# One ordered chain on GpSimd's queue, with a release by ScalarE per step, for the transfers that sum weight blocks in DRAM

## The chip, the cores and the metric

The kernel is one layer of a decoder block and runs on one core of a Trainium2 chip. The metric is the device time of one execution in microseconds. A core has TensorE (PE, matmul), VectorE (DVE), ScalarE (ACT), GpSimd (POOL) and SyncE (SP); each runs its own instructions in order and waits on semaphores for the others. Transfers are issued by an engine (here SP, GpSimd, seldom ScalarE) and carried out by 16 transfer engines that all issuers share.

## The reference

Sequence 512, width 1024, one sequence, float32 throughout. What matters for the change is the second half of the layer, a gated FFN with an inner width of 2816:

```python
    x = x + gate1 * (merged @ w_out)
    h2 = rms_norm(x, norm2_g) * (1.0 + scale2) + shift2
    f_g, f_u = jnp.split(h2 @ w_ffn_in, 2, axis=-1)
    x = x + gate2 * ((jax.nn.silu(f_g) * f_u) @ w_ffn_out)
    return x
```

The gates, scales and shifts come from `silu(c) @ w_ada + b_ada`, one vector of 1024 per section. A final RMSNorm follows.

## The kernel before, in words

**Products.** A float32 product is made of three matmuls on rounded halves: each operand is split into a rounded part (`hi`, made by ScalarE, a copy with rounding) and the rest (`lo`, a subtraction on VectorE). On top of that the larger products are done in the Strassen-Winograd way: seven products of half-size blocks in place of eight, with sums of blocks as operands.

**The first FFN projection** (lines 1623 to 1699) is a loop over `q` from -2 to 17, twenty iterations, each for 256 columns of `w_ffn_in`; even `q` makes the part that goes through SiLU, odd `q` the part that is multiplied by it. An iteration has seven calls of `sprod` (12 matmuls each) into PSUM tiles `R[0]` to `R[3]`. Between them stand, in the order of the code, ScalarE's copies of one PSUM tile into the next (`R[1] <- R[0]`, L1657, `R[2] <- R[1]`, L1670) and into SBUF (`ps`, L1665, L1677), VectorE's sums out of PSUM (L1682, L1685), and the steps that prepare the weights of the next iteration (`s_prep`: `a0`, `a1`, `a2`, `a3` on ScalarE at L1324, L1335, L1345 and L1352; `d0` to `d3` on VectorE at L1327 to L1355). The raw weights of the iteration after next (1 MB, tile `raw`) are loaded by SP at the head of the iteration (`s_issue`, L1298).

**Modulation.** In the iterations with `q` from 1 to 8, `last_mod` does one eighth of the last modulation vector: VectorE multiplies a tile `mraw` of `w_ada` and adds it to `acc` (L175, L177). Every second time SP first loads two such tiles (L205, 512 KB each); they reuse one buffer, so a load starts when the accumulation before it is done.

**Sums of weight blocks.** The second FFN projection is done in seven block products as well, and four of its right operands are sums of blocks of `w_ffn_out`. These sums don't pass through an engine. They are made in DRAM while the first projection runs, in four arrays `wsum[1]` to `wsum[4]`, each cut into `NZ` = 5 blocks of 256x512 (512 KB). For one block `c`, with B(i,j) the block in half i of the rows and half j of the columns, `wsum_steps` (line 292) lists six steps:

1. copy B(0,0) to `wsum[1]` and B(0,1) to `wsum[3]`
2. add B(0,1) to `wsum[1]` and B(1,1) to `wsum[3]`
3. copy `wsum[1]` to `wsum[2]`
4. add B(1,1) to `wsum[2]`
5. copy `wsum[2]` to `wsum[4]`
6. add B(1,0) to `wsum[4]`

That is eight transfers a block. A copy is issued by SP (L307), an addition is an accumulating transfer issued by GpSimd (L305). A step that reads or adds to what an earlier one wrote waits for it on the issuing engine.

**Order around the change.** The program order is the order of the code on every engine. `wstep` (line 318) takes the next entry of the list `wsteps`, if there is one, and calls it; it stands at two places in an iteration, after the third `sprod` (line 1669) and at the end (line 1697), so there are forty places. Before the change the blocks go in pairs: steps 1 of blocks 0 and 1, steps 2 of blocks 0 and 1 and so on (12 places), then blocks 2 and 3 (12 places), then block 4 with an empty place after each step (12 places). Neither SP nor GpSimd waits for the place itself: SP issues a copy when it comes to it in its own queue, and GpSimd an addition when the transfer before it has landed.

**After the loop** the second projection loads its weights through `raw` (L92), partly from `w_ffn_out` and partly from the four arrays, in the order plain, sum 1, sum 2, plain, sum 3, two plain blocks, sum 4, plain. GpSimd loads the gain of the final norm (L1774) and takes powers for the row norms (L1235).

`sm` is a tile of 128x64 for small per-row values; columns 0 to 19 are in use. `cols` holds small constants, loaded at the start.

Of the kernel before, what the change touches and what calls it, by code (L numbers as in the profile page):

```python
# [12 lines left out]
AF = mybir.ActivationFunctionType  # L13
# [15 lines left out]
def block_kernel(ctx: ExitStack, tc: tile.TileContext, x, positions, w_ada, b_ada, w_in,  # L29
# [3 lines left out]
    T, V, A, P, SY = nc.tensor, nc.vector, nc.scalar, nc.gpsimd, nc.sync  # L33
# [116 lines left out]
    cols = base.tile([128, 59], F32, name="cols")  # L150
# [123 lines left out]
    wsum = {n: dram.tile([NZ * 256, 512], F32, name=f"wsum{n}") for n in (1, 2, 3, 4)}  # L274
# [17 lines left out]
    def wsum_steps():  # L292

        def step(c, *moves):
            o = slice(256 * c, 256 * c + 256)

            def fn():
                for n, add, src in moves:
                    if isinstance(src, tuple):
                        k = KZ[src[0]][2 * c] * 128  # L300
                        src = w_ffn_out[k:k + 256, 512 * src[1]:512 * src[1] + 512]
                    else:
                        src = wsum[src][o]
                    if add:
                        P.dma_start(wsum[n][o], src, accum_op=OP.add)  # L305
                    else:
                        SY.dma_start(wsum[n][o], src)  # L307
            return fn

        parts = [[step(c, *m) for m in (  # L310
            ((1, 0, (0, 0)), (3, 0, (0, 1))), ((1, 1, (0, 1)), (3, 1, (1, 1))), ((2, 0, 1),), ((2, 1, (1, 1)),),
            ((4, 0, 2),), ((4, 1, (1, 0)),))] for c in range(NZ)]
        return ([fn for c in (0, 2) for two in zip(parts[c], parts[c + 1]) for fn in two] +
                [fn for one in parts[4] for fn in (one, None)])

    wsteps = wsum_steps()

    def wstep():
        fn = wsteps.pop(0) if wsteps else None
        if fn:  # L320
            fn()
    assert next(mm_, None) is None
    sec_done = []
# [3 lines left out]
    for i in range(4):  # L327
        t = base.tile([128, D], F32, name=f"x{i}", tag=f"X{i}", bufs=1)
# [11 lines left out]
    sm = base.tile([128, 64], F32, name="sm")  # L340
# [1246 lines left out]
    for half in range(2):  # L1587
        o = slice(half * 256, (half + 1) * 256)
# [34 lines left out]
    for q in range(-2, NQ):  # L1623
# [42 lines left out]
        for fn in pre[1]:  # L1666
            fn()
        sprod(R[1], S2_, TB[2], False)
        wstep()
        A.activation(R[2], R[1], AF.Copy)  # L1670
        pre[2][0]()
# [21 lines left out]
        if q == 10:  # L1693
            for b_ in (3, 2):
                mbank[0] = b_
                sec_tasks(one=True)
        wstep()
        if q in (9, 13, NQ - 2):
            a_sum("S1", {9: 0, 13: 2}.get(q, 1))
# [103 lines left out]
    for h in range(2):  # L1803
        hi, lo = get(W_FO[h])
        for tk in range(4):
            o = (Z[h] if tk < 2 else Z[2 + h])[tk % 2]
# [31 lines left out]
    for tk in range(2):  # L1838
        for z in range(2) if tk else (None,):
            c = ALL if z is None else slice(256 * z, 256 * z + 256)  # L1840
            o = Z[1][0] if z is None else (Z[1][1][:, :256], last[:, :256])[z]
            for n_, w in enumerate(ch):
                zmm(o, "S4", 2 + n_, tk, w, c, False, n_ == 2)
            n = c.stop - c.start
# [62 lines left out]
```

## Time and profile before

| What | us |
|---|---|
| runs, median of 3 (lowest, highest) | 832.04 (831.22, 832.65) |
| profiled execution | 831.31 |
| its span | 829.5 |
| TensorE busy in it | 810.3 (98%) |
| VectorE busy | 684.5 (83%) |
| ScalarE busy | 427.0 (51%) |
| GpSimd busy | 126.7 (15%) |

The profile shows one execution. "Busy" leaves out the issuing of transfers on SP, and a busy TensorE is not always at its peak. In a timeline a row has the start and the length in us, the engine, the line of the code, the operation, the tile written and the tiles read, and in brackets the idle time before it with what ended it. In the rows of transfers `x4, 512.0 KB, 11.2` means four issues of 512 KB and the median time of 11.2 us from issue to landing. In the view by stretches each engine has its busy time and, in brackets, the number of instructions; then come the granted clock of TensorE as a share of full speed, the mean busy share of the 16 transfer engines, and GB/s.

### The profile page before, as it was taken

The numbers are of one execution on the slowest core, as the hardware profiler recorded it, in microseconds if no ns is written. First come the engines' busy times: TensorE is split into PE (matmuls) and PEld (weight loads), VectorE is DVE, ScalarE is ACT, GpSimd is POOL, SyncE is SP. The second block draws the span as 40 slices with busy tenths as digits, with TensorE's granted clock in tenths as the row PEclk, the third lists the DMA queues.
The fourth block names the chain that finished last, engine by engine and source line by source line (L and its number), as shares of the span: only waits on it lengthen the run. The fifth ranks groups of instructions, "written<-read, shape, count | busy, mean of one in ns | idle before, by whom it ended". The sixth has DMA issues, their size and how long they took to land.

```text
span 829.5 us, 12872 instructions
## 1 busy us (share of the span) xinstructions
PE 810.3 (98%) x4920; PEld 723.6 (87%) x4920; DVE 684.5 (83%) x1167; ACT 427.0 (51%) x730; POOL 126.7 (15%) x121
## 2 busy tenths in 40 slices
PE   7999999999999999999999999999899999999995
PEld 6889889988888888988888899999899999888784
DVE  7989788798899558886697869899699888897676
ACT  6674444323322236665536586555355556666543
POOL 2060032362353411000000001001000000000001
PEclk9999999999999999999999999999999999999999
DMA  9974352423345652057531409899998863556533
GB/s 296 310 203 118 102 178 77 118 87 101 124 137 176 197 178 77 26 157 243 185 102 50 154 28 257 222 271 295 254 265 208 199 162 125 178 189 195 177 129 126
DMA packets 108477, 138.46 MB, mean 167 GB/s; under 512 B 6480, under 2 KB 77136, under 8 KB 108256
## 3 DMA queue, kind: packets, MB, share of 16 engines
q1 hardware_dynamic: 99872, 120.24, 45.7%
q0 software_dynamic: 7824, 16.59, 10.4%
q8 instruction: 38, 0.62, 0.3%
q10 hardware_dynamic: 720, 0.82, 0.3%
q14 instruction: 23, 0.19, 0.1%
HBM read 135.26 MB, written 23.07 MB: 191 GB/s over the span
## 4 chain that ended last, share of the span: by engine, by line
PE 50%; DVE 18%; DMA 6%; ACT 2%; issue 2%; POOL 0%; POOLq 0%; ACTq 0%; DVEq 0%
PE R L53 6%; PE R L54 6%; PE R L55 6%; DMA mraw<-in_w_ada_dram 6%; PE pfo L55 3%; PE pfo L53 3%; PE pfo L54 3%; DVE acc L177 3%; DVE sco L713 2%; DVE m L709 2%; PE pb L53 2%; PE pb L55 2%; PE pb L54 2%; DVE lo L116 2%; PE po L54 2%
## 5 line engine op out<-in xcount | busy, mean ns | idle before, releaser
L112 ACT ACTIVATE hi<-raw 128x1024 fp32r<-128x1024 f32 (+2 forms) x103 | 107.0, 1040 | 105.3 <-PE pfo L55 34.3
L116 DVE TENSOR_TENSOR lo<-raw,hi 128x1024 fp32r<-128x1024 f32 (+2 forms) x67 | 81.1, 1214 | 29.1 <-ACT hi L112 28.9
L116 POOL TENSOR_TENSOR lo<-raw,hi 128x1024 fp32r<-128x1024 f32 x29 | 73.3, 2531 | 127.9 <-ACT hi L112 122.2
L53 PE MATMUL pb<-h,hi 128*128 128x512 f32 (+1 forms) x192 | 74.6, 389 | 0.0
L54 PE MATMUL pb<-h,hi 128*128 128x512 f32 (+1 forms) x192 | 74.0, 385 | 0.0
L55 PE MATMUL pb<-h,lo 128*128 128x512 f32 (+1 forms) x192 | 74.0, 385 | 0.0
L54 PE MATMUL pfo<-lo,za 128*128 128x512 f32 (+1 forms) x146 | 56.3, 385 | 0.3 <-DVE lo L116 0.3
L55 PE MATMUL pfo<-hi,za 128*128 128x512 f32 (+1 forms) x146 | 56.2, 385 | 0.0
L53 PE MATMUL pfo<-hi,za 128*128 128x512 f32 (+1 forms) x146 | 56.1, 385 | 0.0
L177 DVE SCALAR_TENSOR_TENSOR acc<-mraw,cols,acc 128x512 f32<-128x512 f32 x49 | 39.6, 808 | 18.9 <-DMA mraw<-in_w_ada_dram 17.9
L53 PE MATMUL R<-tb,hi 128*128 128x256 f32 x160 | 45.0, 281 | 2.9 <-ACT R L1670 2.1
L53 PE MATMUL R<-tb,sx 128*128 128x256 f32 x160 | 45.3, 283 | 0.9 <-ACT R L1657 0.8
L54 PE MATMUL R<-tb,sx 128*128 128x256 f32 x160 | 45.1, 282 | 0.0
L55 PE MATMUL R<-tb,sx 128*128 128x256 f32 x160 | 45.0, 281 | 0.0
L55 PE MATMUL R<-tb,lo 128*128 128x256 f32 x160 | 44.9, 281 | 0.0
L54 PE MATMUL R<-tb,hi 128*128 128x256 f32 x160 | 44.7, 279 | 0.0
L305 POOL DMA_DIRECT2D wsum<-in_w_ffn_out_dram x20 | 17.8, 908 | 172.7 <-DMA wsum<-wsum 115.3
L55 PEld LDWEIGHTS pb<-h,lo 128*128 128x128 f32 x192 | 36.0, 187 | 7.3
L54 PEld LDWEIGHTS pb<-h,hi 128*128 128x128 f32 x192 | 36.0, 188 | 6.9
L53 PEld LDWEIGHTS pb<-h,hi 128*128 128x128 f32 x192 | 36.0, 188 | 6.9
L1235 POOL TENSOR_TENSOR sm<-sm,mhalf 128x1 f32<-128x1 f32 x8 | 5.3, 662 | 217.6 <-DVE sm L1234 217.6
L54 PE MATMUL pav<-lo,h 128*128 128x256 f32 x128 | 35.8, 279 | 0.0
(373 smaller groups left out, 2643.6 us busy)
## 6 DMA issues: line engine op xcount, KB each, us to landing
raw<-in_w_ffn_in_dram SPq DMA_DIRECT2D x44, 512.0 KB, 6.5
raw<-in_w_in_dram SPq DMA_DIRECT2D x40, 512.0 KB, 3.8
mraw<-in_w_ada_dram SPq DMA_DIRECT2D x28, 512.0 KB, 4.0
wsum<-in_w_ffn_out_dram POOLq DMA_DIRECT2D x20, 512.0 KB, 9.3
raw<-wsum SPq DMA_DIRECT2D x20, 512.0 KB, 3.7
raw<-in_w_ffn_out_dram SPq DMA_DIRECT2D x18, 512.0 KB, 3.8
s<-in_w_ada_dram SPq DMA_DIRECT2D x30, 256.0 KB, 5.6
wsum<-in_w_ffn_out_dram SPq DMA_DIRECT2D x10, 512.0 KB, 8.6
```

What stands on the lines that cost most here:

```text
L53: T.matmul(o, wh, rh, start=start, stop=False, **kw)
L54: T.matmul(o, wh, rlo, start=False, stop=False, **kw)
L55: T.matmul(o, wlo, rh, start=False, stop=stop, **kw)
L112: A.activation(hi[:, :m], e["raw"][:, :m], AF.Copy)
L116: e["lo"].tensor_sub(lo[:, :m], e["raw"][:, :m], f(hi[:, :m]))
L177: V.scalar_tensor_tensor(o, w, cs[:, j:j + 1], o, op0=OP.mult, op1=OP.add)
L305: P.dma_start(wsum[n][o], src, accum_op=OP.add)
L709: V.max(m8s[i], sco[i])
L713: V.match_replace(out=sco[i], in_to_replace=m8s[i], in_values=sco[i], imm_value=TAKEN)
L1235: P.tensor_tensor(r2[:, tk:tk + 1], r2[:, tk:tk + 1], mhalf[:, :1], op=OP.pow)
```

## The change

Three things are changed in `wsum_steps` and `wstep`:

- The copies are issued by GpSimd, as the additions are. SP has none of these transfers any more.
- The order is one block after the other, six steps each, three steps and then an empty place. The thirty steps take all forty places, the last step the 39th.
- Ahead of each step ScalarE copies a column of 128 values (from `cols`) to a column of `sm` of the step's own, in 20 to 59, and GpSimd copies that column onto itself. GpSimd runs in order, so the step's transfers are issued after ScalarE has come to the step's place.

```diff
                     if add:
                         P.dma_start(wsum[n][o], src, accum_op=OP.add)
                     else:
-                        SY.dma_start(wsum[n][o], src)
+                        P.dma_start(wsum[n][o], src)
             return fn
...
-        return ([fn for c in (0, 2) for two in zip(parts[c], parts[c + 1]) for fn in two] +
-                [fn for one in parts[4] for fn in (one, None)])
+        order = sum(parts, [])
+        return [fn for k in range(0, len(order), 3) for fn in order[k:k + 3] + [None]]
 
     wsteps = wsum_steps()
 
     def wstep():
+
         fn = wsteps.pop(0) if wsteps else None
         if fn:
+            t = sm[:, 20 + len(wsteps):21 + len(wsteps)]
+            A.activation(t, cols[:, 58:59], AF.Copy)
+            P.tensor_copy(t, t)
             fn()
```

## The prediction

> **What bounds the kernel now.** I read the page first, then the matrix engine's time by stretches, then the instructions around the one stretch that is long, and last the transfers in flight there.
>
> ```profile
> PE 810.3 (98%) x4920; PEld 723.6 (87%) x4920; DVE 684.5 (83%) x1167; ACT 427.0 (51%) x730; POOL 126.7 (15%) x121
> ```
>
> TensorE is busy 98% of the span, so an edit can save only the time in which it stands still or runs slowly. The edit is in the twenty-iteration loop of the first FFN projection. I number its iterations 0 to 19 (the loop variable q is two less) and cut the trace at the first matmul of an iteration, the one on the tile `sa`; that of iteration 9 is:
>
> ```profile
> 598.90 0.28 PE L53 MATMUL R<-h,sa 128*128 128x256 f32 x1
> ```
>
> The view by stretches, cut so, for iterations 7 to 10:
>
> ```profile
> core 0: us, PE busy (x) PEld busy (x) DVE busy (x) ACT busy (x) POOL busy (x), PEclk, DMA share, GB/s
> 574.29:584.27 9.98, 9.98 (x86) 9.98 (x85) 9.23 (x13) 5.84 (x11) 2.65 (x3) 1.00 1.05 203
> 584.27:598.90 14.63, 11.74 (x86) 11.24 (x85) 8.09 (x14) 4.76 (x9) 0.48 (x1) 0.88 0.99 298
> 598.90:609.95 11.05, 10.25 (x86) 10.05 (x85) 10.64 (x14) 7.02 (x13) 1.28 (x2) 1.00 0.95 198
> 609.95:619.89 9.94, 9.94 (x86) 9.94 (x85) 9.45 (x15) 4.91 (x9) 0.88 (x1) 1.00 0.90 313
> ```
>
> A clean iteration takes 9.96 us (the mean of the first and last row). Iteration 8 takes 14.63 and iteration 9 11.05, with the same matmul count: 4.67 + 1.09 = **5.76 us** lost, part of it at a granted clock of 0.88. This is the loop's only stall on which the change can act. Who was late is in the timelines of ScalarE, TensorE and VectorE:
>
> ```profile
> 590.80 1.06 ACT L1335 ACTIVATE sx<-raw 128x1024 fp32r<-128x1024 f32 x1 [3.06 <-DMA raw<-in_w_ffn_in_dram]
> 591.76 0.37 ACT L1670 ACTIVATE R<-R 128x256 f32<-128x256 f32 x1
> 592.18 0.38 PE L53 MATMUL R<-tb,hi 128*128 128x256 f32 x1 [2.08 <-ACT R L1670]
> 592.49 0.49 DVE L175 TENSOR_SCALAR acc<-mraw,cols 128x512 f32<-128x512 f32 x1 [6.37 <-DMA mraw<-in_w_ada_dram]
> 595.73 1.06 ACT L1345 ACTIVATE sx<-raw 128x1024 fp32r<-128x1024 f32 x1 [3.61 <-DVE raw L1331]
> ```
>
> Two loads came late. ScalarE waited 3.06 us for a weight tile (`raw`), and the PSUM copy that TensorE needs (L1670) stood behind that wait; VectorE waited 6.37 us for a modulation tile (`mraw`), and through L1331 and L1345 that held ScalarE again. The chain of waits goes the same way; its longest piece in the loop is this transfer (start, length):
>
> ```profile
> 576.81 15.65 DMA mraw<-in_w_ada_dram
> ```
>
> What shared the transfer engines with it is in the timelines of SP's queue and GpSimd, and in the times to landing:
>
> ```profile
> 564.73 3.02 SPq L307 DMA_DIRECT2D wsum<-in_w_ffn_out_dram  x4
> 573.48 1.59 SPq L1298 DMA_DIRECT2D raw<-in_w_ffn_in_dram  x2
> 576.81 1.19 SPq L205 DMA_DIRECT2D mraw<-in_w_ada_dram  x2
> 572.97 0.88 POOL L305 DMA_DIRECT2D wsum<-in_w_ffn_out_dram  x1 [18.22 <-DMA wsum<-in_w_ffn_out_dram]
> 577.18 0.88 POOL L305 DMA_DIRECT2D wsum<-in_w_ffn_out_dram  x1 [0.42 <-issue]
> ```
>
> ```profile
> wsum<-in_w_ffn_out_dram POOLq DMA_DIRECT2D x4, 512.0 KB, 11.2
> raw<-in_w_ffn_in_dram SPq DMA_DIRECT2D x2, 512.0 KB, 13.8
> mraw<-in_w_ada_dram SPq DMA_DIRECT2D x2, 512.0 KB, 16.1
> mraw<-in_w_ada_dram SPq DMA_DIRECT2D x2, 512.0 KB, 10.9
> mraw<-in_w_ada_dram SPq DMA_DIRECT2D x2, 512.0 KB, 9.1
> ```
>
> The first three rows are issues between 571.5 and 579 us, the last two the loads of `mraw` in iterations 3 and 5. Two blocks of the weights' sums run side by side, so four copies and then four accumulating transfers (2 MB) fall together, and in iteration 7 those four meet 1 MB of weights and 1 MB of `mraw`. In iterations 3 and 5, beside two accumulating transfers, `mraw` lands in 9 to 11 us and no iteration is long.
>
> **The change part by part.** Three edits are made: the order (one block after the other, three steps in every four places), the queue (20 copies leave SP for GpSimd), and the gate (per step a 128x1 copy on ScalarE and one on GpSimd).
>
> Order: a step now holds two transfers at most, each waits for its predecessor, and a block takes 8 places, or four iterations: 4 x 9.96 = 39.8 us. What meets the `mraw` of iteration 7 is the second block's fourth step, one accumulating transfer, instead of four. How late may the loads be? VectorE was free for `mraw` 6.37 us before 592.49, at 586.12, or 9.3 us after its issue; the weight tile must let L1335 and L1670 (1.06 + 0.37) end by the fifth of seven products of iteration 8, 584.27 + 4/7 x 9.96 = 589.96, so it has to land by 588.5, some 14 us after its issue. With 9.1 to 10.9 us for `mraw`, VectorE is at most 1.6 us late, and of its 6.37 us here 2.8 never reached ScalarE (3.61); the weight tile has room. From below: nothing is saved if landing stays at 13.8 and 16.1; from above: all 5.76 us. I take all of it, since the traffic is below that of iterations 3 and 5.
>
> Queue: SP loses 20 issues and its waits for the accumulations; it is not on the path but it issues the weights. GpSimd gains 20 issues, priced by those it makes now.
>
> ```profile
> L305 POOL DMA_DIRECT2D wsum<-in_w_ffn_out_dram x20: 872/881/1307, 506.8 to 677.3; - x20
> L486 ACT ACTIVATE G<-modS,cols x8: 342/344/346, 15.8 to 51.7; 128x1 f32<-128x1 f32 x8
> L352 POOL TENSOR_SCALAR sm<-sm x4: 192/231/695, 6.5 to 12.3; 128x1 f32<-128x1 f32 x4
> ```
>
> 20 x 0.88 = 17.6 us of GpSimd, which has only this chain to do in the loop. Nothing that anybody waits for soon is queued behind it: the load of the final norm's gain is, and is used only in the last products.
>
> Gate: 30 x 0.34 = 10.3 us on ScalarE, 30 x 0.23 = 6.9 us on GpSimd. ScalarE has 4 to 5 us idle in a clean iteration (5.84 of 9.98 busy), mostly ahead of copies out of PSUM, so I cost most of it at nothing; without that cover it is up to 10.3 us. The tight place is the end of an even iteration, where ten of the gates stand ahead of L1657:
>
> ```profile
> 576.22 0.37 ACT L1657 ACTIVATE R<-R 128x256 f32<-128x256 f32 x1
> ```
>
> That copy ends at 576.59, and the third product needs it at 574.29 + 2/7 x 9.96 = 577.14: 0.55 us of room, 0.2 after a gate. In iterations 9 and 11, where VectorE's modulation work has added up, I estimate 0.2 us lost each: **0.4 us**; bounds 0 and 10.3.
>
> Does ScalarE's write of a column of `sm` wait for GpSimd's copy of the column before? Then ScalarE would hang behind the whole chain. Two rows of another stage, columns of the same tile, VectorE's reduction and GpSimd's power:
>
> ```profile
> 469.77 0.16 DVE L1234 TENSOR_REDUCE sm<-ss 128x1 f32<-128x5 f32 x1 [0.18 <-ACT rt L1227]
> 469.68 1.41 POOL L1235 TENSOR_TENSOR sm<-sm,mhalf 128x1 f32<-128x1 f32 x2 [92.29 <-DVE sm L1234]
> ```
>
> The reduction writes its column while GpSimd works on the neighbour, so columns don't wait for each other, and I cost this at nothing.
>
> GpSimd's copies may slow VectorE. The rows for that are from the LayerNorm, the same instruction beside GpSimd's subtraction and without it:
>
> ```profile
> 168.85 6.72 POOL L116 TENSOR_TENSOR lo<-raw,hi 128x1024 fp32r<-128x1024 f32 x2
> 170.06 3.25 DVE L901 SCALAR_TENSOR_TENSOR vg<-vg,sm,lnb 128x1024 f32<-128x1024 f32 x1
> 176.68 1.28 DVE L901 SCALAR_TENSOR_TENSOR vg<-vg,sm,lnb 128x1024 f32<-128x1024 f32 x1
> ```
>
> VectorE took 2 us more beside 1024 elements per row; beside one element the loss is at most GpSimd's 0.23 us, 12 gates in the eight modulation iterations making 2.8 us, spread over 80 us in which VectorE idles about 0.5 us an iteration. I take 0. The Trainium skill (GPSIMD Engine Reference, section 1, Specifications) says that the two engines share SBUF interfaces and contend where VectorE has two SBUF inputs. The pair of rows agrees, and by the rule VectorE's subtractions in the loop are exposed; it speaks against this gate, and by it the sum would be up to 2.8 us worse.
>
> Does the chain end in time? Its hops, from the nearest transfers: two copies, two copies under load, one copy, two accumulations, one accumulation:
>
> ```profile
> wsum<-in_w_ffn_out_dram SPq DMA_DIRECT2D x2, 512.0 KB, 7.7
> wsum<-wsum SPq DMA_DIRECT2D x2, 512.0 KB, 9.7
> wsum<-wsum SPq DMA_DIRECT2D x1, 512.0 KB, 5.5
> wsum<-in_w_ffn_out_dram POOLq DMA_DIRECT2D x2, 512.0 KB, 8.2
> wsum<-in_w_ffn_out_dram POOLq DMA_DIRECT2D x1, 512.0 KB, 6.6
> ```
>
> A block is 7.7 + 8.2 + 5.5 + 6.6 + 5.5 + 0.9 for the last issue = 34.4 us, less than the 39.8 of its places, so the gates set the pace. The first starts in the middle of iteration 0, at 598.90 - 4.67 - 9 x 9.96 + 3/7 x 9.96 = 509 us, and the fifth 4 x 39.8 us later, near 668. The loads of the sums are here:
>
> ```profile
> 711.09 28.12 SPq L92 DMA_DIRECT2D raw<-wsum  x10
> ```
>
> The second sum's last block is the tenth load, near 736 now and 731 after; it is ready four hops after the start, at 668 + 28 = 696. A block could take 48 us before that load is late. Price 0; if each hop cost the 9.7 to 11.2 us of the crowded rows, 49 to 57 us a block, it would be late.
>
> Sum: 5.76 - 0.4 = 5.36 us saved, against the profiled execution's 831.31 us (span 829.5, 1.8 around it): 825.95. The median of the runs is 0.73 higher, 832.04, and the forecast for it **826.7 us**. What follows the loop is TensorE-bound and moves forward whole.
>
> **The rivals.**
>
> *The collision moves.* Block three's pair of copies and pair of accumulations fall into iterations 8 to 10, with the last `mraw` in 9; copies now share engines with weights instead of standing behind them in SP's queue. For it: the transfer engines' share is 0.90 to 1.05 in the rows by stretches. Against it: iterations 3 and 5 carried such pairs. If iteration 8's 4.67 us come back there, 1.09 is saved: 831.0. The Trainium skill (DMA: Bandwidth & Descriptors, Queues, rings and completion order) says that each engine alternates between the queues that hold work, packet by packet. By that rule the weights get half of an engine while GpSimd's queue has work, where now they keep it ahead of copies issued after them; the rule is this rival's mechanism, and the price stays the one worked out from the rows.
>
> *The gates are not covered*, slower than before: each 0.34 us of ScalarE lands ahead of a PSUM copy for which TensorE waits, 30 x 0.34 = 10.3 us, less 5.76: 836.6. It decides once ScalarE's room ahead of L1657 and L1670 is under 0.34 us. Against it: 0.55 us of room measured in one of the late iterations.
>
> *The chain is late*, slower: with hops of 10.3 us a block takes 51.5 us, the last sum is 4 x (51.5 - 48) = 14 us late, less 5.36: 840.7. Against it: only bursts of four reached such times.
>
> *The gates don't gate.* GpSimd waits for landings anyway; with gates passed early a block takes 34.4 us, the burst is gone all the same: 826.
>
> **How the numbers follow.** Forecast 62%, collision moved 17%, gates uncovered 8%, chain late 6%, no gating 7%. About 0.2% (1.7 us) can be told from no change, so faster means under 830.4. The forecast and the last rival are faster (69%), the moved collision lies across the bound, 5% faster and 12% the same, and the other two are slower: 74, 12 and 14%. The range runs from the whole 5.76 with a run's scatter of 0.9 us (825.4) to the moved collision (831.2): 62 + 7 and most of 17, some 81%.
>
> **What would show it.** Right: iterations 8 and 9 at 10 us and clock 1.00, `mraw` of iteration 7 landing in 9 to 11 us, ScalarE's wait ahead of L1335 gone, block pace near 40 us, no wait of SP for `wsum`. Wrong: a long iteration elsewhere between 3 and 11, TensorE waiting for L1657 in odd iterations, or loads of `wsum` waiting for GpSimd's transfers after 700 us.

## The result and the profile after

| What | before | after |
|---|---|---|
| runs, median (lowest, highest), us | 832.35 (831.22, 833.37), 4 runs | 825.23 (823.90, 825.97), 4 runs |
| profiled execution, us | 831.31 | 825.28 |
| its span, us | 829.5 | 823.4 |
| TensorE busy in it, us | 810.3 | 808.5 |

The ratio is 0.9913, with a 95% interval from 0.9895 to 0.9931: the change is faster by some 7 us. The forecast was 826.7, and 825.23 lies 0.17 below the low end of the range.

The iterations 7 to 11 of the changed kernel, in the view by stretches with the columns of the prediction:

```profile
573.85:583.83 9.98, 9.98 (x86) 9.98 (x85) 9.22 (x13) 6.50 (x14) 1.85 (x3) 1.00 1.03 311
583.83:593.77 9.94, 9.94 (x86) 9.94 (x85) 9.77 (x15) 4.87 (x9) 2.72 (x4) 1.00 0.95 244
593.77:603.75 9.98, 9.98 (x86) 9.98 (x85) 8.96 (x13) 6.50 (x14) 3.15 (x4) 1.00 1.03 258
603.75:613.69 9.94, 9.94 (x86) 9.94 (x85) 8.52 (x14) 4.29 (x9) 1.83 (x3) 1.00 0.76 236
613.69:624.66 10.97, 10.23 (x86) 10.02 (x85) 10.47 (x14) 7.70 (x17) 2.36 (x4) 1.00 0.80 198
```

Iterations 8 and 9, which took 14.63 and 11.05 us, are clean at full clock. Iteration 11, clean before, is 1.0 us long. The landing times say why the first two are clean. These rows are the transfers issued between 571.5 and 579 us in the changed kernel (the same stretch as in the prediction):

```profile
raw<-in_w_ffn_in_dram SPq DMA_DIRECT2D x2, 512.0 KB, 6.1
mraw<-in_w_ada_dram SPq DMA_DIRECT2D x2, 512.0 KB, 7.4
wsum<-in_w_ffn_out_dram POOLq DMA_DIRECT2D x1, 512.0 KB, 6.5
wsum<-wsum POOLq DMA_DIRECT2D x1, 512.0 KB, 6.9
```

One accumulation and one copy stand beside the loads, in place of four accumulations, and `raw` lands in 6.1 us (13.8 before) and `mraw` in 7.4 (16.1).

The long iteration 11 goes back to iteration 9. The landings of the transfers issued between 593 and 599 us (medians of the two tiles; VectorE needs the first, after 10.8 us), and then the rows of the timeline from there to TensorE's wait:

```profile
wsum<-in_w_ffn_out_dram POOLq DMA_DIRECT2D x2, 512.0 KB, 12.2
mraw<-in_w_ada_dram SPq DMA_DIRECT2D x2, 512.0 KB, 12.3
```

```profile
595.39 1.82 POOL L305 DMA_DIRECT2D wsum<-in_w_ffn_out_dram  x2
596.02 0.89 SPq L205 DMA_DIRECT2D mraw<-in_w_ada_dram  x2
606.85 1.54 DVE L177 SCALAR_TENSOR_TENSOR acc<-mraw,cols,acc 128x512 f32<-128x512 f32 x2 [1.25 <-DMA mraw<-in_w_ada_dram]
617.03 0.36 ACT L1661 ACTIVATE R<-R 128x256 f32<-128x256 f32 x1
617.45 0.39 PE L53 MATMUL R<-tb,sx 128*128 128x256 f32 x1 [0.74 <-ACT R L1661]
```

The third block's two accumulations go out 0.6 us ahead of the last `mraw`; VectorE waits 1.25 us for it in iteration 10, is late to the end of that iteration, and ScalarE's copy at L1661 (L1657 before the change) comes late for TensorE. This is the rival "the collision moves", at the place that it named and at about a fifth of its price (1.0 us in place of 4.67).

Where the 6.1 us between the two spans lie follows from the first and the last iteration's first matmul, before and then after:

```profile
504.64 0.29 PE L53 MATMUL R<-h,sa 128*128 128x256 f32 x1
700.50 0.28 PE L53 MATMUL R<-h,sa 128*128 128x256 f32 x1
```

```profile
504.19 0.29 PE L53 MATMUL R<-h,sa 128*128 128x256 f32 x1
695.30 0.28 PE L53 MATMUL R<-h,sa 128*128 128x256 f32 x1
```

The loop between them took 195.86 us and takes 191.11: 4.75 saved, which is the stall of 5.76 less the 1.0 of iteration 11. The code ahead of the loop is the same in both and came out 0.45 shorter. What follows the last iteration's start, 829.5 - 700.50 = 129.0 us, is now 823.4 - 695.30 = 128.1, so 0.9 shorter, and that was not foreseen. The gain lies behind the issue of the last store of the output, which is here, before and then after:

```profile
824.31 0.35 ACTq L1717 DMA_DIRECT2D out_dram<-xo  x1
```

```profile
819.41 0.34 ACTq L1721 DMA_DIRECT2D out_dram<-xo  x1
```

From there to the end of the span it is 5.19 us before and 3.99 after: 1.2 us. I call this stretch the tail. The stores of the output land 2.1 to 2.8 us after their issue in both kernels, so the difference arises after the last landing.

### The profile page after: what moved, and what is told of

Same layout as the page of the kernel before. It is cut to its first block, busy times and chain, and to the rows that moved or that the text cites. A ratio compares the mean times of both kernels' runs of the same rounds, so it can differ in the third digit from the quotient of the medians.

```text
span 823.4 us, 12920 instructions
## 1 busy us (share of the span) xinstructions
PE 808.5 (98%) x4920; PEld 722.0 (88%) x4920; DVE 684.9 (83%) x1167; ACT 427.7 (52%) x760; POOL 156.5 (19%) x171
## 4 chain that ended last, share of the span: by engine, by line
PE 51%; DVE 19%; DMA 5%; ACT 2%; issue 2%; POOL 0%; POOLq 0%; ACTq 0%; DVEq 0%
PE R L53 6%; PE R L54 6%; PE R L55 6%; DMA mraw<-in_w_ada_dram 5%; PE pfo L55 3%; PE pfo L54 3%; PE pfo L53 3%; DVE acc L177 3%; DVE sco L717 2%; DVE m L713 2%; PE pb L53 2%; PE pb L55 2%; PE pb L54 2%; DVE lo L116 2%; PE po L54 2%
## 5 line engine op out<-in xcount | busy, mean ns | idle before, releaser
L116 POOL TENSOR_TENSOR lo<-raw,hi 128x1024 fp32r<-128x1024 f32 x29 | 73.0, 2521 | 128.1 <-ACT hi L112 122.4
L177 DVE SCALAR_TENSOR_TENSOR acc<-mraw,cols,acc 128x512 f32<-128x512 f32 x49 | 39.8, 813 | 19.6 <-DMA mraw<-in_w_ada_dram 18.6
L324 POOL COPY sm<-sm 128x1 f32<-128x1 f32 x30 | 18.9, 631 | 117.0 <-ACT sm L323 116.9
```

Source lines behind the costliest of these rows:

```text
L116: e["lo"].tensor_sub(lo[:, :m], e["raw"][:, :m], f(hi[:, :m]))
L177: V.scalar_tensor_tensor(o, w, cs[:, j:j + 1], o, op0=OP.mult, op1=OP.add)
L324: P.tensor_copy(t, t)
```

## The experiments

The theory: the burst of four accumulations in iteration 7 made the stall, so the order earns the gain. The main rivals are that taking the copies off SP's queue earns it, or that the gates do, by pacing. The result raised two more questions, what makes iteration 11 long and what makes the tail shorter. Each set of runs has its own runs of the kernel before beside it; the ratio is to those.

**The kernel before, once more.** No edit.

> The kernel before once more, to see what differs from one profiled execution to the next. If the gain is only the loop's stall, its iterations 8 and 9 are long again by 5 to 6 us in sum, and what lies outside the loop (before it, and between the last issue of a store and the end) scatters by about 1 us either way. If the stall itself changes from execution to execution, iterations 8 and 9 differ from 14.6 and 11.1 us by more than 1 us. Ratio to before 1.00.

Measured: 832.06 us, ratio 1.0001 [0.9992, 1.0011]. Its profile has the stall again, in the same place, by 6.2 us where the first had 5.76:

```profile
584.95:599.90 14.95, 11.41 (x86) 11.20 (x85) 9.30 (x15) 4.73 (x8) 0.43 (x1) 0.86 0.97 288
599.90:611.02 11.12, 11.12 (x85) 11.12 (x85) 9.51 (x13) 6.44 (x12) 1.32 (x2) 0.89 1.00 234
```

The stall belongs to the program, and its size differs by tenths between executions. The tail is 5.2 us again.

**The queue alone.** The old order, no gates.

```diff
-                        SY.dma_start(wsum[n][o], src)
+                        P.dma_start(wsum[n][o], src)
```

> Only the queue: the copies are issued by GpSimd, in the order of before, without the gate. Theory (bursts of four transfers are what makes weights and mraw late): the bursts stay and start earlier, since GpSimd is free from about 490 us on, so long iterations stay and move towards iterations 3 to 6; 828 to 834 us. Rival (it was the copies in SP's queue that held up the weights): no long iteration, 825 to 827 us.

Measured: 837.69 us, ratio 1.0075 [1.0046, 1.0104]: slower than before, and above both ranges. With nothing ahead of them in GpSimd's queue the copies start before the loop, and the second burst, four copies and then four accumulations, meets the first `mraw` of the loop, issued at 534.9. Iterations 4 and 5, and the landings of what was issued from 532 to 552 us:

```profile
544.51:561.03 16.52, 11.67 (x87) 11.27 (x85) 9.29 (x15) 4.74 (x8) 3.67 (x5) 0.88 1.09 263
561.03:575.76 14.73, 12.94 (x85) 12.74 (x85) 9.51 (x13) 6.40 (x12) 2.32 (x3) 0.79 1.07 316
```

```profile
wsum<-in_w_ffn_out_dram POOLq DMA_DIRECT2D x9, 512.0 KB, 12.3
raw<-in_w_ffn_in_dram SPq DMA_DIRECT2D x4, 512.0 KB, 18.9
mraw<-in_w_ada_dram SPq DMA_DIRECT2D x2, 512.0 KB, 19.7
```

Iteration 8 is clean and 9 takes 10.34 us. So the stall goes where the burst goes, and the queue alone earns nothing in the loop. The tail, though, is 4.0 us: of the two differences between the profiles after and before, this one belongs to the queue.

**The order alone.** Copies on SP, no gates.

```diff
-        return ([fn for c in (0, 2) for two in zip(parts[c], parts[c + 1]) for fn in two] +
-                [fn for one in parts[4] for fn in (one, None)])
+        order = sum(parts, [])
+        return [fn for k in range(0, len(order), 3) for fn in order[k:k + 3] + [None]]
```

> Only the order: one block after the other, copies on SP, no gate. Theory: no burst of four, but SP now stands waiting for the accumulations of the block it is in, with the weights behind it in its queue; long iterations in many places, waits of SP for wsum of 5 us and more, 833 to 850 us. Rival (the order alone gives the gain): 825 to 828 us.

Measured: 828.69 us, ratio 0.9953 [0.9938, 0.9968], in neither range. The waits of SP for `wsum` that the theory named are there, 53.3 us in sum, but they make no row of long iterations: iterations 8 and 9 take 9.94 and 9.98 us, and iteration 11 alone is long, with 10.78. That last loss has another source than in the changed kernel. SP stands behind a copy that waits for an accumulation, and so issues the last `mraw` at 600.29, 4.3 us later than there; it lands in 7.5 us:

```profile
599.72 0.48 SPq L307 DMA_DIRECT2D wsum<-wsum  x1
600.29 1.05 SPq L205 DMA_DIRECT2D mraw<-in_w_ada_dram  x2
```

Behind the loop it loses more: ScalarE waits 2.8 us longer for a weight tile than in the changed kernel. The first two rows are SP's queue, the third ScalarE; the fence after it is ScalarE's like row in the changed kernel:

```profile
695.61 0.48 SPq L307 DMA_DIRECT2D wsum<-wsum  x1
696.19 6.49 SPq L92 DMA_DIRECT2D raw<-in_w_ffn_out_dram  x4
711.15 1.06 ACT L112 ACTIVATE hi<-raw 128x1024 fp32r<-128x1024 f32 x1 [7.27 <-DMA raw<-in_w_ffn_out_dram]
```

```profile
708.05 1.06 ACT L112 ACTIVATE hi<-raw 128x1024 fp32r<-128x1024 f32 x1 [4.45 <-DMA raw<-in_w_ffn_out_dram]
```

SP waits for an accumulation before it issues the last copy at 695.61, and four loads of the second projection stand behind that wait: they go out at 696.2, 701.3, 701.8 and 702.3, in the changed kernel at 693.5, 699.6, 700.0 and 702.2. So with this order the queue does matter, in the loop and for the block whose copies come last. The tail is 5.2 us here.

**Order and queue, no gates.**

```diff
         if fn:
-            t = sm[:, 20 + len(wsteps):21 + len(wsteps)]
-            A.activation(t, cols[:, 58:59], AF.Copy)
-            P.tensor_copy(t, t)
             fn()
```

> Order and queue without the gate: GpSimd runs the chain at the pace of its landings, from about 490 us. Theory (two transfers in flight are few enough, wherever they fall): at most one long iteration of under 2 us, 824.5 to 827 us. Rival (the gate is what keeps the transfers off the loads of mraw): long iterations of 2 us and more, 828 us and more. If the gate itself costs ScalarE what iteration 11 lost (1.0 us), this is 1 us faster than the change, though the place of the pairs moves too.

Measured: 825.27 us, ratio 0.9914 [0.9899, 0.9929], the same as the change. The chain's last accumulation is issued at 667.57 us, 35 earlier than with the gates, and nobody gains or loses by it. Iteration 11 is 11.05 us without a single gate, so the gates don't make it long. What stands beside the last `mraw` here is one accumulation and two plain copies, and it lands in 11.4 us, about as late as beside the pair of accumulations. No run tells an accumulating transfer from a plain one in what it costs a load.

**Half the burst.** The kernel before, where block 3, the fourth, leaves out step 2, two of the four accumulations; sums 1 and 3, and what is made from them, lack an addend there.

```diff
+                    if add and c == 3 and len(moves) == 2:
+                        continue
```

> The kernel before with two of the four accumulating transfers of iteration 7 left out (the second step of block 3, so sums 1 and 3 lack an addend there). Theory (four accumulations beside 2 MB of loads are one burst too many): iterations 8 and 9 take 10 us each, mraw of iteration 7 lands in 8 to 11 us; iteration 11 then loses up to 1 us as in the change; 826 to 827.5 us. Rival (the loads are late for another reason, such as SP's queue): iteration 8 stays over 12 us.

Measured: 826.58 us, ratio 0.9936 [0.9921, 0.9951], in the theory's range; iteration 9 is not clean, though, and iteration 11, at 9.98 us, is. Iterations 8 and 9, and the landings from 571.5 to 579 us:

```profile
584.13:594.47 10.34, 10.19 (x87) 9.99 (x86) 8.08 (x14) 4.75 (x9) 0.55 (x1) 1.00 0.81 305
594.47:605.52 11.05, 10.24 (x86) 10.04 (x85) 10.63 (x14) 7.07 (x13) 1.21 (x2) 1.00 0.96 209
```

```profile
wsum<-in_w_ffn_out_dram POOLq DMA_DIRECT2D x2, 512.0 KB, 10.1
raw<-in_w_ffn_in_dram SPq DMA_DIRECT2D x2, 512.0 KB, 11.5
mraw<-in_w_ada_dram SPq DMA_DIRECT2D x2, 512.0 KB, 11.8
```

Two accumulations fewer take 4.3 us from iteration 8, with order and queue as before and no gates. This shows the cause of the large stall directly. What two accumulations still do, 0.4 + 1.1 us, is of the kind that iteration 11 of the changed kernel shows: there too a pair meets an `mraw`.

**The third block later.** The change with three empty places ahead of the third block, so that its pair of accumulations no longer meets the last `mraw`.

```diff
-        return [fn for k in range(0, len(order), 3) for fn in order[k:k + 3] + [None]]
+        early, late = order[:12], order[12:]
+        return ([fn for k in range(0, 12, 3) for fn in early[k:k + 3] + [None]] + [None] * 3 +
+                [fn for k in range(0, 18, 3) for fn in late[k:k + 3] + [None] * (k < 9)])
```

> The change with three more empty places ahead of the third block, so that its pairs start after the last mraw has landed. Theory A (the loss of iteration 11 comes from VectorE, which does eight modulation iterations in a row and falls behind): iteration 11 still takes 10.7 to 11.1 us, 825.2 us. Theory B (it comes from the pair of accumulations that made the last mraw land in 12.3 us): iteration 11 takes 10.0 us, 824.2 us.

Measured: 826.16 us, ratio 0.9931 [0.9914, 0.9948], above the time of either theory. The last `mraw` lands in 6.2 us, and iteration 11 is clean:

```profile
mraw<-in_w_ada_dram SPq DMA_DIRECT2D x2, 512.0 KB, 6.2
```

```profile
614.90:624.88 9.98, 9.98 (x87) 9.98 (x86) 9.22 (x13) 7.26 (x16) 1.11 (x4) 1.00 1.05 254
```

This is theory B's iteration: with the pair away the load lands early and nothing is lost. It is one profile, and a second profile of the unedited change, below, is clean too, so this run supports the cause without showing it alone. The us gained in the loop doesn't show in the time, whose interval is wider than it.

**Modulation spread wider.** The change with the eighths of the modulation at other iterations, the later ones two later.

```diff
+    MODQ = (1, 2, 3, 5, 6, 7, 9, 10)
...
-        if 1 <= q <= 8:
-            last_mod(q - 1)
-        if q == 9:
+        if q in MODQ:
+            last_mod(MODQ.index(q))
+        if q == 11:
             last_gate()
-        if q == 10:
+        if q == 12:
```

> The change with the modulation work in q = 1, 2, 3, 5, 6, 7, 9, 10 in place of 1 to 8, and its last steps two iterations later, so that VectorE can catch up twice. Theory A (VectorE falls behind): all iterations 10.0 us but the one with the four extra matmuls (10.9), 824.2 us. Theory B: an iteration with a loss of about 1 us stays, 825.2 us.

Measured: 825.52 us, ratio 0.9924 [0.9909, 0.9938]. Iteration 11 is clean here too, but iteration 13 takes 10.78 us, with no load late: a sum of 1.22 us on VectorE (L1578) now stands right behind modulation work there, which is the likely reason. Nothing is gained, and neither theory is told from the other.

**Thirty and twenty small loads on SP.** The tail is short wherever SP issues fewer transfers, so the change with 1 KB transfers added to the loop on SP's queue: thirty, or twenty, which is the count of before. The lines for twenty (for thirty the condition is left out):

```diff
+            k = len(wsteps)
+            if k >= 10:
+                SY.dma_start(pad[k:k + 1, :], x[k:k + 1, 0:256])
```

> The change with thirty further transfers of 1 KB from SP in the loop, so that SP's program is again as long as before. Theory (the 1.2 us that the change saves between the last store's issue and the end are a fetch of program code that SP no longer needs there): 5.2 us from the last store's issue to the end in place of 4.0, with one packet of an instruction queue in them, 826.4 us. Rival (that end depends on which queue carries the sums' copies): 4.0 us, 825.2 us.

> The change plus twenty 1 KB transfers on SP in the loop, so that SP issues exactly as many transfers as before the change. If the 1.2 us at the end hangs on where SP's last instructions lie in its code (a late fetch of 8 KB), the tail is 5.2 us again and a fetch packet stands after the last store has landed; the loop is as in the change and the time is 825 to 826.4. If the tail hangs on what SP copies in the loop (the sums of the weights), it stays at 4.0 us and the time is 823.6 to 825.2.

Measured: 823.59 us, ratio 0.99 [0.9884, 0.9917], with thirty, and 824.16, ratio 0.9911 [0.9898, 0.9925], with twenty. The tails are 4.0 and 3.8 us: the number of SP's transfers, and with it where its last instructions lie in its code, doesn't set it. The time with thirty is below both forecasts. The loop is clean with thirty. With twenty the pair meets `mraw` again, and VectorE waits longer for it than in the change:

```profile
603.66:613.89 10.23, 10.22 (x87) 10.01 (x86) 8.38 (x14) 4.14 (x9) 1.66 (x3) 1.00 0.79 245
613.89:625.01 11.12, 10.23 (x86) 10.03 (x85) 10.61 (x14) 7.83 (x17) 2.40 (x4) 1.00 0.80 200
```

```profile
607.19 1.54 DVE L177 SCALAR_TENSOR_TENSOR acc<-mraw,cols,acc 128x512 f32<-128x512 f32 x2 [1.68 <-DMA mraw<-in_w_ada_dram]
```

**The change, once more, and the kernel before with eight small loads.** The same lines as above with `k >= 22`, in the kernel before.

> The changed kernel once more, to see what of its profile comes again. If the long iteration 11 is the moved collision, it is again 10.9 to 11.0 us, with mraw of iteration 9 landing in about 12 us. If it was chance, it is 9.96. The tail from the last store's issue to the end of the span is 4.0 us by every theory. Time 825.2, from 824.2 to 826.2.

> The kernel before plus eight 1 KB transfers on SP in the loop, nothing else. If the tail hangs on where SP's last instructions lie in its code, eight more move the boundary ahead of the last store's wait, the tail is 4.0 us, and the time 830.8. If it hangs on SP's part in the sums of the weights, the tail stays at 5.2 us and the time is 832.0. The stall of iterations 8 and 9 stays between 5 and 6.5 us by both.

Measured: the change 824.11 us, ratio 0.9915 [0.9901, 0.9928], beside 830.93 of before; the kernel before with eight loads 832.54, ratio 1.002 [1.0011, 1.0029]. Iterations 10 and 11 of the change, in this second profile of the same program, and VectorE's row for `mraw`:

```profile
603.96:613.90 9.94, 9.94 (x86) 9.94 (x85) 9.77 (x15) 4.85 (x9) 1.83 (x3) 1.00 0.83 246
613.90:623.88 9.98, 9.98 (x86) 9.98 (x85) 9.23 (x13) 7.30 (x16) 1.87 (x4) 1.00 0.84 226
```

```profile
605.74 1.53 DVE L177 SCALAR_TENSOR_TENSOR acc<-mraw,cols,acc 128x512 f32<-128x512 f32 x2
```

No bracket stands behind the last row: `mraw` landed just in time, and the iteration is clean. By the expectation's own words the long iteration 11 was chance. With the rows of the change beside it, it is a load at the edge of being late, which one execution of the same program paid for and another did not. In the kernel before with eight loads, the stall of iteration 8 is the largest seen (with iteration 9, of 11.05 us, 7.6 us are lost, where 5 to 6.5 were expected), and the tail stays: the store is issued 5.2 us before the span's end at 830.7:

```profile
583.56:600.07 16.51, 12.26 (x86) 11.65 (x85) 8.11 (x14) 4.60 (x9) 0.65 (x1) 0.90 0.91 279
```

```profile
825.47 0.34 ACTq L1721 DMA_DIRECT2D out_dram<-xo  x1
```

The tails of all thirteen profiles sort by one thing. With the copies on SP's queue they are 5.2 us in four of them and in a fifth, with half the burst, 4.6; with the copies on GpSimd's queue they are 3.8 to 4.0 in all eight. That moving the copies makes the tail shorter is shown, by the run of the queue alone; what in the end of the program takes the 1.2 us is open. A late fetch of code doesn't sort the tails: with the eight loads no packet of an instruction queue stands between the store's issue and the end, and the tail is 5.2 us; with the thirty loads one stands there, and it is 4.0. Whether it is SP's program or GpSimd's, which the moved copies change as well, was not tested; half the burst, where only GpSimd issues less, hints at a part of GpSimd's.

## Why the prediction was right, and where it was not

**The bound and the cause of the stall: right.** The loop's stall came from four accumulations beside two megabytes of loads. Half of them taken away takes 4.3 us from iteration 8, and the queue alone moves burst and stall together to iterations 4 and 5.

**The order: right.** `mraw` of iteration 7 was to land in 9 to 11 us and landed in 7.4; iterations 8 and 9 are clean, and ScalarE's wait ahead of L1335 is gone. "No wait of SP for `wsum`" was no sign: the profile before lists none either.

**"VectorE is at most 1.6 us late", taken as absorbed: wrong.** The limit itself held, 9.3 us after the issue; in iteration 9 it is 605.60 - 596.02 = 9.6. But being late is not absorbed. In four kernels the last `mraw` came late: in the order alone, where SP issued it late, in the change, in order and queue without gates, and in the change with twenty small loads. VectorE waited 1.16, 1.25, 1.41 and 1.68 us, and iterations 10 and 11 were long by 0.8, 1.0, 1.1 and 1.4 us together: all but the first 0.3 is lost, whatever made the load late. The rows of the first and the third are these:

```profile
607.41 1.54 DVE L177 SCALAR_TENSOR_TENSOR acc<-mraw,cols,acc 128x512 f32<-128x512 f32 x2 [1.16 <-DMA mraw<-in_w_ada_dram]
```

```profile
607.71 1.54 DVE L177 SCALAR_TENSOR_TENSOR acc<-mraw,cols,acc 128x512 f32<-128x512 f32 x2 [1.41 <-DMA mraw<-in_w_ada_dram]
```

The second profile of the change shows why: in iteration 10 VectorE is busy for 9.77 of the 9.94 us. The "2.8 that never reached ScalarE" in the kernel before was no slack: ScalarE was itself late there, by its 3.06 us for `raw`. In iteration 7 the error did no harm, since the load was early. In iteration 9 it let the sum leave out the moved collision, which a rival held.

**The gates, 0.4 us: no such loss shows.** Without the gates the time is the same, 825.27 us beside 825.23, though the pairs fall elsewhere then. Their rows, with duration as lowest, median, highest in ns, and then, from the view of GpSimd's copy, what that copy waited for:

```profile
L323 ACT ACTIVATE sm<-cols x30: 184/190/198, 508.4 to 701.0; 128x1 f32<-128x1 f32 x30
L324 POOL COPY sm<-sm x30: 178/444/1220, 508.7 to 701.2; 128x1 f32<-128x1 f32 x30
```

```profile
  ACT sm L323: 116.9, 28
```

A gate costs ScalarE 0.19 us, not 0.34, and fits into the 0.55 us ahead of the copy. The gates do gate: GpSimd waited 116.9 us for them, 28 of 30 times. The rule of the Trainium skill that GpSimd and VectorE contend (GPSIMD Engine Reference, section 1, Specifications) would have made the sum up to 2.8 us worse. The trace shows no such loss: the clean iterations with gates take 9.94 to 9.98 us, and iteration 11 is as long without gates; GpSimd's own copy of one element per row, from 0.18 to 1.22 us, is what varies.

**The queue, priced at nothing: the step that failed.** A copy costs GpSimd 0.52 to 0.59 us, less than the 0.88 taken. But "what follows the loop is TensorE-bound and moves forward whole" put the effect of the moved copies on the end of the program at nothing, without a row for it: with the copies on GpSimd the tail is 1.2 us shorter. With a tail 1.2 us longer the median would have been some 826.4 us, inside the range. Besides, without the queue the new order would have cost some 3 us behind the loop (the order alone took 827.7 - 695.8 = 131.9 us from the last iteration's start, the kernel before 129.0). The prediction did not see that, because it priced the queue by GpSimd's issues and left out what the new order does to SP's queue.

**The chain: right.** First copies of the first and the last block, the last accumulation, and the loads of the sums:

```profile
508.90 1.17 POOL L307 DMA_DIRECT2D wsum<-in_w_ffn_out_dram  x2
670.13 1.16 POOL L307 DMA_DIRECT2D wsum<-in_w_ffn_out_dram  x2
703.07 0.87 POOL L305 DMA_DIRECT2D wsum<-in_w_ffn_out_dram  x1 [1.64 <-DMA wsum<-wsum]
```

```profile
710.40 25.17 SPq L92 DMA_DIRECT2D raw<-wsum  x10
```

A block takes (670.13 - 508.90) / 4 = 40.3 us, where 39.8 was said; no load waits for it.

**The sum and the range.** Of the 6.1 us between the two spans the loop gave 4.75, where 5.36 was forecast, the tail 1.2, the rest of the stretch behind the loop took 0.3, and the code ahead of the loop, unchanged, gave 0.45 (its end lies between 503.4 and 505.3 us over all profiles). The loop gave 0.6 us less than forecast, and the parts outside it gave 1.4 that the sum didn't hold, 0.45 of them from code that the change doesn't touch; that the errors have opposite signs is luck. The other half of the miss, which is 1.5 us in all, lies in the 0.73 us between the profiled execution and the median before: they were added to the forecast, but the changed kernel's profiled execution lies 0.05 above its median. A stall whose size differs between executions, and which the change takes away, would do that; no run shows it. The low end was set at the whole 5.76 of one execution. That is not the most that can be saved: the stall was 6.2 us in a second profile, and the tail came on top.

## What to carry to other kernels

Transfers that no engine needs soon still set the time if several of them run beside loads that are needed soon: spread them so that few stand beside a load with a deadline (here one with a copy did no harm, two were at the edge), and look at each load with a deadline, not only at the one that stalls today. On an engine that is busy 98% of an iteration, a load that comes more than 1 us late costs nearly all of that, even if the profile of before seems to show slack there. Take transfers that wait for others off the queue that carries the next stage's loads, and price each edit of a change by itself, since one may cover the loss of another.

## What the runs showed of the hardware

The landing time of a 512 KB load grew with the transfers of the sums beside it: `mraw` of iteration 7 landed in 16.1 us beside four, in 11.8 beside two and in 7.4 beside one with a copy. The last `mraw` landed in 12.3 us beside two accumulations (the change) and in 11.4 beside one and two copies (order and queue, no gates). The busy share of the transfer engines doesn't show the difference; it was 1.05 in iteration 7 before and 1.03 after, while they moved 203 and 311 GB/s. The end of the program took 3.8 to 4.0 us from the last store's issue with the copies on GpSimd's queue, with up to thirty other transfers on SP's, and 5.2 with them on SP's (4.6 with half the burst). TensorE's granted clock fell with the long standstills: 0.88 and 0.79 in the two iterations of 16.52 and 14.73 us, and 0.89 in one of 11.12 us in which TensorE never stood still, right behind one of 14.95 us at 0.86. It was 1.00 in all clean ones shown.
